# A second home for the shifted copy of g, convolution diagonals loaded from memory, and state scalars emitted inside the MLP

## The chip, the core and the metric

The kernel runs on one core of a Trainium2 chip. The metric is the device time of one execution in microseconds (us). Three runs of the kernel before took 1066.11, 1067.0 and 1065.13 us, median 1066.11. TensorE (PE) does the matrix products, VectorE (DVE) and ScalarE (ACT) the elementwise work, GpSimd (POOL) fills and small jobs; SP issues nearly all DMA.

## What is computed

Two blocks run one after the other on a sequence of 256 tokens with 1024 channels, in float32. The first block has two hybrid layers (sliding-window attention beside retention, gates, and an MLP with squared ReLU). The second has an "even" mixer (block attention and pooling) and an "odd" mixer, in which a state-space branch stands beside a convolution branch. Only the odd mixer is touched by what follows:

```python
def odd_mixer(h, w_in, ...):
    z = h @ w_in
    su, gc, ca, cb, gd = jnp.split(z, ...)          # 512 channels each
    y = s5_ssm(su, ...)                             # state branch
    ya, yb = jnp.split(y @ glu_w + glu_b, 2, axis=-1)
    ssm_out = ya * jax.nn.sigmoid(yb) * jax.nn.silu(gc)
    conv_out = conformer_conv(ca, cb, dw, ln_g, ln_b, pw) * jax.nn.silu(gd)
    return jnp.concatenate([ssm_out, conv_out], axis=-1) @ w_out

def conformer_conv(a, gl, dw, ln_g, ln_b, pw):
    g = a * jax.nn.sigmoid(gl)
    c = causal depthwise convolution of g, 31 taps per channel
    return silu(layernorm(c) * ln_g + ln_b) @ pw
```

## The kernel before

All weights stream through SP in 164 chunks, nearly all of 1 MB (`raw0` to `raw163`, three buffers, `fetch`, line 315). Each chunk is cut in two halves of 128x1024; ACT casts a half to `hi` (line 336) and DVE makes the rest `lo` (line 337), five buffers each, and every product is three matmuls of `hi` and `lo` parts. The Tile framework puts the instructions in order on each engine; code under `tc.high_priority(-N)` is moved towards the rear. Each engine, and SP with its DMA queue, works strictly in its own order.

The odd mixer takes the last 165 us and the chunks 147 to 163: `su` (147, 148), `cb` and `ca` of the two channel halves (149 to 152), `gc` and `gd` (153 to 156, all written to banks named `og`), the GLU weights (157 for `gb`, 158 for `ga`), then the output and point weights (159 to 163).

The convolution is done by TensorE. The gated input g is written into the tile `big` in two halves of 256 channels (line 1361). `strip(p)` (line 1326) makes a copy `g4[p]` in which the four partition groups hold g shifted by 0, 8, 16 and 24 tokens, with 16 DMAs of 65.8 KB each from SBUF to SBUF (line 1331). The copy of half 0 lies in the room of `pwc`, which the state branch reads until its output matrices `Q` are written (`s5_outputs`, line 1249, 16 small ACT operations, line 1207). The copy of half 1 lies in the room of `E`, which `states(0)` to `states(3)` (line 1292) read. `convolve(p)` (line 1341) then multiplies each channel group with diagonal 32x32 matrices of taps, 128 matmuls a half (line 1349), into a bank `cq`. The diagonals are made in eight pieces by POOL (`taps`, line 1334), three buffers, from the tap vectors in `pv` and an identity table `e32`.

`states(q)` is a DVE chain of products, two scans (line 1308, with a mask `Mt` from ACT and POOL) and products again, for four groups q; its results `wall` are read by the state output matmuls `ys` (line 1410), which follow the matmuls `ys` of the inner part (line 1403). Then come the means for the layer norm (`mu`, line 1390), `gb`, `ga` and the output product `yo`.

The large tiles named `xs` take turns in two rooms of 16 KB a partition: the normalized input of the odd mixer (read by `su` to `og`), `BT`, `Q`, and later `is_` and `fs` (inputs of the GLU and output products). The bank tag `sm` has four banks; the four `vb` banks that `states` reads hold all of them until each is read.

`after_mixer` (line 1519) closes the pool of the layer and emits the scalars of the state branch at low priority. It is called at line 830, ahead of the MLP of layer 1.

Of the kernel before, what the change touches and what calls it, by code (L numbers as in the profile page):

```python
# [152 lines left out]
def pack_weights(cs, inp):  # L153
# [3 lines left out]
    for blocks, n in zip(cs, w):  # L157
# [14 lines left out]


_PV = [("g_mix", 16), ("g_mlp", 16), ("g_final", 8), ("pre", 16), ("post", 16), ("pscale", 4), ("d", 4),
       ("glub", 8), ("dw", 16 * KP), ("lng", 4), ("lnb", 4), ("sinks", 16)]
PVO = {}
_o = 0
for _n, _w in _PV:
# [6 lines left out]
def strips(dw):  # L185

    t = np.zeros((4 * KP, 512), np.float32)
    t[:CONVK] = dw
    return t.reshape(4, KP, 4, 4, 32).transpose(0, 4, 2, 1, 3).reshape(P, 16 * KP)


def pack_vectors(inp):
    def v(a):
        return np.asarray(a, np.float32).reshape(-1, P).T

    cols = [v(inp["g_mix"]), v(inp["g_mlp"]), v(inp["g_final"]), v(inp["pre_norm_g_2"]), v(inp["post_norm_g_2"]),
            v(inp["e_pool_scale_2"]), v(inp["o_d_2"]), v(inp["o_glu_b_2"]),
            strips(inp["o_dw_2"][0]),
            v(inp["o_ln_g_2"]), v(inp["o_ln_b_2"]),
            np.broadcast_to(inp["sinks"].reshape(1, 16), (P, 16))]  # L200
    return np.ascontiguousarray(np.concatenate(cols, axis=1))


# [11 lines left out]
    return np.ascontiguousarray(np.concatenate(cols, axis=1))  # L215


_CT = [("ident", 128), ("mask0", 128), ("maske", 256), ("ecos", 64), ("esin", 64), ("blk", 128), ("icnt", 64), ("e32", 32)]
_MT = [("rcos", 256), ("rsin", 128), ("acos", 128), ("asin", 64), ("mask1", 256), ("dm", 1024)]
CTO = {}  # L220
_o = 0
# [8 lines left out]
def tables():  # L230
    t = np.zeros((P, NCT), np.float32)

    def put(name, a):
        t[:, CTO[name][0]:CTO[name][1]] = np.asarray(a, np.float64).reshape(P, -1)

    f32 = np.float32
    pos = np.arange(S, dtype=f32)

    def rope(inv):
        ang = (pos[:, None] * inv.astype(f32)[None, :]).astype(f32).astype(np.float64)  # L240
        c, s = np.cos(ang), np.sin(ang)
        return [a.reshape(NT, P, -1).transpose(1, 0, 2) for a in (np.concatenate([c, c], axis=1), s)]

    put("ident", np.eye(P))
    c, s = rope((10000.0 ** (-(np.arange(32) / 32.0))).astype(f32))
    put("acos", c)
    put("asin", s)
    theta = (1.0 / (10000.0 ** np.linspace(0.0, 1.0, 64))).astype(f32)
    c, s = rope(theta)
    put("rcos", c)  # L250
    put("rsin", s)
    c, s = rope((500000.0 ** (-(np.arange(0, 32, 2) / 32.0))).astype(f32))
    put("ecos", c)
    put("esin", np.concatenate([-s, s], axis=2))
    lg = np.log(1.0 - 2.0 ** (-5.0 - np.arange(4)))
    j, i = np.arange(P)[:, None], np.arange(P)[None, :]
    dm = np.zeros((P, 2, 4, P))
    for h in range(4):
        dm[:, 0, h] = np.where(i >= j, np.exp(lg[h] * np.maximum(i - j, 0)), 0.0)
        dm[:, 1, h] = np.exp(lg[h] * (i + P - j))  # L260
    put("dm", dm)
    q, k = np.arange(P)[:, None], np.arange(P)[None, :]
    put("mask0", np.where(k <= q, 0.0, NEG))
    k = np.arange(2 * P)[None, :]
    rel = q + P - k
    put("mask1", np.where((rel >= 0) & (rel < P), 0.0, NEG))
    put("maske", np.where(rel >= 0, 0.0, NEG))
    cnt = np.stack([np.minimum(np.arange(S) + 1, w) for w in (2, 4, 8, 16)])
    put("icnt", np.broadcast_to((1.0 / cnt)[None, :, :16], (P, 4, 16)))
    blk = np.zeros((P, 4, 32))  # L270
    for r in range(4):
        blk[32 * r:32 * r + 32, r] = 1.0
    put("blk", blk)
    put("e32", np.tile(np.eye(32), (4, 1)))
    return t


# [3 lines left out]
def build(ctx, tc, w, xin, pv_in, ct_in, s5_in, pg_in, out, parts=(0, 1, "e", "o"), dbg=None):  # L281
# [329 lines left out]
    def layer(l, xh, xl, norm, after_mixer, done):  # L611
# [215 lines left out]
            split_pair(xh2, xl2, x, "g_mlp", l * KT, p)  # L827
            n2.add(s)
        dump(f"xa{l}", x)
        after_mixer()  # L830


        def up(j, hook=None):
            hi, lo = chunk()
# [50 lines left out]

        bs = [up(0), up(1, square)]
        cur = up_out(bs[0])
        for j in range(16):
            if j + AHEAD < 16:
                bs.append(up(j + AHEAD))  # L890
            nxt = up_out(bs[j + 1]) if j < 15 else None
            if not accs:
                accs += [[bank("acc", f"dn{t}{h}") for h in range(2)] for t in range(NT)]
            hi, lo = chunk()
            if j < 15:
                for kk in range(2):
                    for t in range(NT):
                        for h in range(2):
                            down(j, cur, t, h, kk, hi, lo)
            else:  # L900
                ys = {}
                for h in range(2):
                    for t in range(NT):
                        for kk in range(2):
                            down(j, cur, t, h, kk, hi, lo)
                        ys[h, t] = w2("dny")
                        A.activation(ys[h, t], accs[t][h], AF.Copy, scale=r2[0][:, t:t + 1])
                        if h and t == 0:
                            back(0, [ys[0, 0], ys[0, 1]])
                back(1, [ys[1, 0], ys[1, 1]])  # L910
            cur = nxt
# [348 lines left out]
    def odd(pool, xh, xl, n, s5, tabs5):  # L1260
# [26 lines left out]
                                 start=True, stop=True)  # L1287
                vbs.append(vb)

        pg = pool.tile([P, D], F32, name="pg", tag="cd", bufs=1)  # L1290

        def states(q):
            vb = vbs[q]
            wt = wall[:, q]
            W.append(wt)
            ec, es = (E[:, a, 4 * q:4 * q + 4, :].rearrange("p r c -> p (r c)")[:, None, :].to_broadcast([P, 2, 4 * NC])
                      for a in range(2))
            tb = pool.tile([P, 2, 4 * NC], F32, name="tb", tag="tb", bufs=2)
            tt(wt, vb, ec, M)
            tt(tb, vb, es, M)  # L1300
            tt(wt[:, 0], wt[:, 0], tb[:, 1], AD)
            tt(wt[:, 1], wt[:, 1], tb[:, 0], SU)
            m = w2("Mt")[:, 0:4 * NC].rearrange("p (r c) -> p r c", r=4)
            A.copy(m, mL[:, 4 * q:4 * q + 4, None].to_broadcast([P, 4, NC]))
            G.memset(m[:, :, 0:1], 0.0)
            mf = m.rearrange("p r c -> p (r c)")
            for a in range(2):
                V.tensor_tensor_scan(wt[:, a], mf, wt[:, a], 0.0, M, AD)
            tb = pool.tile([P, 2, 4 * NC], F32, name="tb", tag="tb", bufs=2)
            tt(tb, wt, es, M)  # L1310
            tt(wt, wt, ec, M)
            tt(wt[:, 0], wt[:, 0], tb[:, 1], SU)
            stt(wt[:, 1], wt[:, 1], -1.0, tb[:, 0], M, SU)
# [11 lines left out]

        def strip(p):

            g4[p] = s5["pool"].tile([P, 2, 4, GS + 1], F32, name="g4", tag=("pwc", "E")[p], bufs=1)
            for s in range(4):
                for r in range(4):  # L1330
                    nc.sync.dma_start(g4[p][32 * s:32 * s + 32, :, r, 0:GS],
                                      g[32 * r:32 * r + 32, 2 * p:2 * p + 2, KP * s:KP * s + GS])

        def taps(q, h):
            n = 2 * KP
            o = PVO["dw"] + (2 * q + h) * n
            tap[q, h] = pool.tile([P, n, 32], F32, name="taps", tag="taps", bufs=3)
            G.tensor_tensor(tap[q, h], pv[:, o:o + n, None].to_broadcast([P, n, 32]),
                            C("e32")[:, None, :].to_broadcast([P, n, 32]), op=M)

        def convolve(p):
            b = bank("sm", "cq").rearrange("p (j t) -> p j t", j=2)
            for j in range(2):
                q = 2 * p + j
                for k in range(KP):
                    if k % 4 == 0:
                        taps(q, k // 4)
                    for r in range(4):
                        T.matmul(b[32 * r:32 * r + 32, j, :], tap[q, k // 4][:, 4 * (k % 4) + r, :],
                                 g4[p][:, j, r, k:k + S], start=k == 0, stop=k == KP - 1)  # L1350
            A.copy(cv[:, 2 * p:2 * p + 2, :], b)

        for p in range(2):
# [9 lines left out]
            if p == 0:  # L1363
                inputs()
                with tc.high_priority(-LOWW):
                    Q = s5_outputs(pool, s5)
                G.dma_start(pg, bass.AP(tensor=pg_in.tensor, offset=pg_in.offset, ap=[[0, P], [1, D]]))
        for i, d in enumerate((gc, gd)):
            with tc.high_priority(-LOWW):
                states(i)  # L1370
            for p in range(2):
                silu_gate(d[:, 2 * p:2 * p + 2, :], t_pair("acc", "og", xh, xl), R, 0.25)
        convolve(0)
        states(2)
        convolve(1)
        states(3)

        fh, fl, fs = twin("fs")
        ih, il, is_ = twin("is_")

        hb = pool.tile([P, 16], F32, name="hb")
# [40 lines left out]
        for p, b in enumerate(t_quad("acc", "gb", ih, il)):  # L1422
            for j in range(2):
                n = 2 * p + j
                th = w2("gth")[:, 0:S]
                A.activation(th, b[:, j, :], AF.Tanh, scale=0.5, bias=hb[:, 4 + n:5 + n])
                stt(gc[:, n, :], th, 1.0, gc[:, n, :], AD, M)
        gas = t_quad("acc", "ga", ih, il, hook=lambda: later.append(nv.rstd()))
        r3 = later.pop()
        for p, b in enumerate(gas):  # L1430
# [108 lines left out]
    for p in range(4):  # L1539
        n.add(x[:, 2 * p:2 * p + 2, :])  # L1540
    fetch()
    nc.sync.dma_start(pv[:, NG:], pv_in[:, NG:])
    nr = CTO["mask1"][0] - NCC
    nc.sync.dma_start(tabs[1][:, 0:nr], ct_in[:, NCC:NCC + nr])
    nc.sync.dma_start(ct, ct_in[:, 0:NCC])
# [117 lines left out]
```

## Time and profile before

| What | Value |
|---|---|
| median of three runs | 1066.11 us |
| time of the profiled execution | 1064.91 us |
| its span, first to last instruction | 1063.1 us |
| TensorE busy | 1025.0 us, 96% of the span |
| VectorE, ScalarE, GpSimd busy | 759.9, 547.1, 22.7 us |
| mean granted TensorE clock | 0.989 |
| moved by DMA | 179.05 MB, mean 168 GB/s |

The profiled execution is 1.2 us below the median, and 1.8 us of it lie outside the span. A row "A <- B: us, times, longest" in the view of waits says that A stood idle until B ended. In timelines and in the chain of waits the first column is the start, the second the time until the end of the piece, which may hold several equal instructions (xN).

### The profile page before, as it was taken

Reading aid. Unit: us, or ns where it says so; the run is one execution under the profiler, and the core shown is the slowest. Engines: PE = TensorE matmul, PEld = TensorE weight load, DVE = VectorE, ACT = ScalarE, POOL = GpSimd, SP = SyncE. Lnnn points to the kernel's source line nnn. Section 1 sums busy time; section 2 is a strip of 40 time slices with the busy share of each in tenths; the row PEclk is TensorE's granted clock in tenths of the full one; section 3 lists DMA queues with packets and bytes.
Section 4 is the critical chain, followed back from the end, with each engine's and each line's share of the span. In section 5 each row is a group of like instructions: output and inputs, shape, how many; then the busy total and the mean of one; then the engine's idle time right before and its main releaser. Section 6 shows DMA issues by size and latency. Waiting matters only on the chain.

```text
span 1063.1 us, 16059 instructions
## 1 busy us (share of the span) xinstructions
PE 1025.0 (96%) x6404; PEld 882.6 (83%) x6404; DVE 759.9 (71%) x1306; ACT 547.1 (51%) x844; POOL 22.7 (2%) x24
## 2 busy tenths in 40 slices
PE   7999999999999999999999999999999998995796
PEld 5887888988888888887888988888878998994595
DVE  6768656785666659478566999965677886879085
ACT  6545653554445455547544554445475557562052
POOL 0000000000000000000000000000000030012000
PEclk9999999999999999999999999999999999998799
DMA  9654445455555545544445555555545443444121
GB/s 333 227 175 154 159 138 180 163 195 196 181 198 176 198 171 186 198 158 153 153 149 193 171 194 198 176 199 179 198 153 182 151 159 121 150 139 176 35 80 40
DMA packets 29274, 179.05 MB, mean 168 GB/s; under 512 B 3600, under 2 KB 5776, under 8 KB 8592
## 3 DMA queue, kind: packets, MB, share of 16 engines
q1 hardware_dynamic: 28624, 176.44, 48.2%
q8 instruction: 50, 0.82, 0.3%
q0 software_dynamic: 288, 1.07, 0.3%
q10 hardware_dynamic: 288, 0.52, 0.1%
q14 instruction: 24, 0.20, 0.1%
HBM read 174.82 MB, written 1.05 MB: 165 GB/s over the span
## 4 chain that ended last, share of the span: by engine, by line
PE 91%; DVE 4%; ACT 2%; DMA 1%; issue 1%; SPq 1%; DVEq 0%; ACTq 0%
PE up L842 11%; PE ng L406 6%; PE ng L404 6%; PE ng L405 6%; PE up L843 6%; PE dn L865 5%; PE dn L864 5%; PE dn L866 5%; PE gate L404 3%; PE gate L406 3%; PE gate L405 3%; PE yb L406 1%; PE yb L404 1%; PE yb L405 1%; DVE lo L337 1%
## 5 line engine op out<-in xcount | busy, mean ns | idle before, releaser
L337 DVE TENSOR_TENSOR lo<-raw,hi 128x1024 fp32r<-128x1024 f32 (+1 forms) x331 | 399.1, 1210 | 188.8 <-ACT hi L336 187.2
L336 ACT CAST hi<-raw 128x1024 fp32r<-128x1024 f32 (+1 forms) x331 | 342.6, 1039 | 313.1 <-PE dn L866 81.7
L842 PE MATMUL up<-xs,hi 128*128 128x512 f32 x512 | 182.0, 398 | 0.8 <-DVE xs L465 0.8
L843 PE MATMUL up<-xs,lo 128*128 128x256 f32 x512 | 143.6, 280 | 0.0
L842 PEld LDWEIGHTS up<-xs,hi 128*128 128x128 f32 x512 | 96.2, 188 | 24.4 <-DVE xs L465 1.2
L404 PE MATMUL ng<-hi,xs 128*128 128x512 f32 x272 | 108.4, 399 | 8.2 <-ACT xs L464 8.2
L405 PE MATMUL ng<-lo,xs 128*128 128x512 f32 x272 | 107.0, 393 | 0.0
L406 PE MATMUL ng<-hi,xs 128*128 128x512 f32 x272 | 106.7, 394 | 0.1
L864 PE MATMUL dn<-hi,uph 128*128 128x512 f32 x256 | 100.1, 391 | 0.0
L865 PE MATMUL dn<-lo,uph 128*128 128x512 f32 x256 | 99.9, 390 | 0.0
L866 PE MATMUL dn<-hi,upl 128*128 128x512 f32 x256 | 99.6, 389 | 0.0
L843 PEld LDWEIGHTS up<-xs,lo 128*128 128x128 f32 x512 | 96.7, 189 | 1.0
L404 PEld LDWEIGHTS ng<-hi,xs 128*128 128x128 f32 x272 | 51.6, 190 | 18.9 <-ACT xs L464 8.7
L406 PEld LDWEIGHTS ng<-hi,xs 128*128 128x128 f32 x272 | 51.3, 189 | 11.8 <-DVE xs L465 1.0
L405 PEld LDWEIGHTS ng<-lo,xs 128*128 128x128 f32 x272 | 51.7, 190 | 10.6
L864 PEld LDWEIGHTS dn<-hi,uph 128*128 128x128 f32 x256 | 48.1, 188 | 10.5
L866 PEld LDWEIGHTS dn<-hi,upl 128*128 128x128 f32 x256 | 48.1, 188 | 10.2
L865 PEld LDWEIGHTS dn<-lo,uph 128*128 128x128 f32 x256 | 48.1, 188 | 8.9
L404 PE MATMUL gate<-hi,xs 128*128 128x512 f32 x128 | 51.6, 403 | 0.0
L406 PE MATMUL gate<-hi,xs 128*128 128x512 f32 x128 | 49.9, 390 | 0.0
L405 PE MATMUL gate<-lo,xs 128*128 128x512 f32 x128 | 49.9, 390 | 0.0
L850 ACT COPY upa<-up 128x256 f32<-128x256 f32 x64 | 23.7, 370 | 47.8 <-PE up L843 47.8
(382 smaller groups left out, 1920.5 us busy)
## 6 DMA issues: line engine op xcount, KB each, us to landing
raw<-w_dram SPq DMA_DIRECT2D x161, 1024.0 KB, 4.9
raw<-w_dram SPq DMA_DIRECT2D x9, 256.0 KB, 5.6
g<-big SPq DMA_DIRECT2D x32, 65.8 KB, 2.0
x<-x_dram SPq DMA_DIRECT2D x4, 256.0 KB, 5.7
ctm<-ct_dram SPq DMA_DIRECT2D x1, 640.0 KB, 10.1
sp<-s_dram POOLq DMA_DIRECT2D x1, 536.0 KB, 4.0
pg<-pg_dram POOLq DMA_DIRECT2D x1, 512.0 KB, 3.7
out_dram<-xn SPq DMA_DIRECT2D x2, 256.0 KB, 2.0
```

The source lines that it names most:

```text
L336: A.copy(hi[:, s], raw[:, rs])
L337: V.tensor_tensor(lo[:, s], raw[:, rs], hi[:, s].bitcast(F32), op=OP.subtract)
L404: T.matmul(b[t], xh[:, k, ts], hi[:, ws], start=f, stop=False)
L405: T.matmul(b[t], xh[:, k, ts], lo[:, ws], start=False, stop=False)
L406: T.matmul(b[t], xl[:, k, ts], hi[:, ws], start=False, stop=e)
L842: T.matmul(bs[i], hi[:, ws], xs2[:, k], start=k == 0, stop=False, skip_group_check=True)
L843: T.matmul(bs[i][:, 1, :], lo[:, ws], xh2[:, k, :], start=False, stop=k == KT - 1, skip_group_check=True)
L850: A.copy(u[:, j, :], b[:, 0, :])
L864: T.matmul(accs[t][h], th[:, kk, tk], hi[:, ws], start=f, stop=False)
L865: T.matmul(accs[t][h], th[:, kk, tk], lo[:, ws], start=False, stop=False)
L866: T.matmul(accs[t][h], tl[:, kk, tk], hi[:, ws], start=False, stop=e)
```

## The change

The second copy of g gets a tile of its own, `g4`, in the pool of the odd mixer; the room comes from the three buffers of diagonals and one of the two buffers `tb`, which go. The diagonals come ready-made from memory, behind the vectors in `pv_dram`: four loads of 512 KB. They lie in the old room of `sp` (q=0), in that of `cd` (q=1), and in one of the two `xs` rooms (q=2 and 3), and are issued by POOL, POOL, SP and ACT. The row `pg`, which lay in the room of `cd`, is loaded behind the convolution. `fs` is allocated later. The call of `after_mixer` stands behind the first products of the MLP.

```diff
@@ strips: taps on the diagonals of 32x32 blocks
-    return t.reshape(4, KP, 4, 4, 32).transpose(0, 4, 2, 1, 3).reshape(P, 16 * KP)
+    t = t.reshape(4, KP, 4, 4, 32).transpose(0, 2, 1, 3, 4)
+    z = np.zeros((4, 32, 4, KP, 4, 32), np.float32)
+    for c in range(32):
+        z[:, c, ..., c] = t[..., c]
+    return z.reshape(P, 512 * KP)
@@ layer
         dump(f"xa{l}", x)
-        after_mixer()
...
         bs = [up(0), up(1, square)]
         cur = up_out(bs[0])
+        after_mixer()
@@ states (twice)
-            tb = pool.tile([P, 2, 4 * NC], F32, name="tb", tag="tb", bufs=2)
+            tb = pool.tile([P, 2, 4 * NC], F32, name="tb", tag="tb", bufs=1)
@@ strip
-            g4[p] = s5["pool"].tile([P, 2, 4, GS + 1], F32, name="g4", tag=("pwc", "E")[p], bufs=1)
+            n = 2 * 4 * (GS + 1)
+            if p == 0:
+                t = s5["pool"].tile([P, n], F32, name="g4", tag="pwc", bufs=1)
+            else:
+                t = pool.tile([P, n], F32, name="g4", tag="g4", bufs=1)
+            g4[p] = t.rearrange("p (j r t) -> p j r t", j=2, r=4)
@@ taps
-        def taps(q, h):
-            n = 2 * KP
-            o = PVO["dw"] + (2 * q + h) * n
-            tap[q, h] = pool.tile([P, n, 32], F32, name="taps", tag="taps", bufs=3)
-            G.tensor_tensor(tap[q, h], pv[:, o:o + n, None].to_broadcast([P, n, 32]),
-                            C("e32")[:, None, :].to_broadcast([P, n, 32]), op=M)
+        def taps():
+            n = KP * P
+            late = acts.tile([P, 4 * n], F32, name="taps", tag="xs", bufs=2)
+            for q in range(4):
+                if q < 2:
+                    home, tag = ((s5["pool"], "sp"), (pool, "cd"))[q]
+                    t = home.tile([P, n], F32, name="taps", tag=tag, bufs=1)
+                else:
+                    t = late[:, (q - 2) * n:(q - 1) * n]
+                (G, G, nc.sync, nc.scalar)[q].dma_start(t, pv_in[:, NPV + q * n:NPV + q * n + n])
+                tap[q] = t.rearrange("p (n c) -> p n c", c=32)
@@ odd, from the first half of g on
-                G.dma_start(pg, bass.AP(tensor=pg_in.tensor, offset=pg_in.offset, ap=[[0, P], [1, D]]))
...
+        taps()
         convolve(0)
         states(2)
         convolve(1)
         states(3)
-        fh, fl, fs = twin("fs")
+        pg = pool.tile([P, D], F32, name="pg", tag="cd", bufs=1)
+        G.dma_start(pg, bass.AP(tensor=pg_in.tensor, offset=pg_in.offset, ap=[[0, P], [1, D]]))
         ih, il, is_ = twin("is_")
...
+        fh, fl, fs = twin("fs")
         gas = t_quad("acc", "ga", ih, il, hook=lambda: later.append(nv.rstd()))
```

The order of the SP queue in the odd mixer before, from the last `gd` chunk on; `g4_8660` is the copy of half 0, `g4_8857` that of half 1:

```order
L325 DMA raw156_8952<-w_dram 128x2048
L325 DMA raw157_9030<-w_dram 128x2048
L1331 DMA g4_8660<-big_8533 32x2x263 x16
L325 DMA raw158_9093<-w_dram 128x2048
L325 DMA raw159_9509<-w_dram 128x2048
L325 DMA raw160_9581<-w_dram 128x2048
L325 DMA raw161_9672<-w_dram 128x2048
L1331 DMA g4_8857<-big_8533 32x2x263 x16
L325 DMA raw162_9729<-w_dram 128x2048
L325 DMA raw163_9763<-w_dram 128x2048
```

and the same place of the same queue after the change, with `g4_8659` for half 0, `g4_8855` for half 1 and the diagonals of q=2:

```order
L327 DMA raw156_8950<-w_dram 128x2048
L1335 DMA g4_8659<-big_8532 32x2x263 x16
L1335 DMA g4_8855<-big_8532 32x2x263 x16
L327 DMA raw157_9028<-w_dram 128x2048
L327 DMA raw158_9091<-w_dram 128x2048
L1348 DMA taps_9154<-pv_dram 128x1024
L327 DMA raw159_9499<-w_dram 128x2048
L327 DMA raw160_9572<-w_dram 128x2048
L327 DMA raw161_9663<-w_dram 128x2048
```

Both copies of g now stand ahead of the GLU weights (157, 158), and the diagonals of q=2 stand behind these.

TensorE's order before, from the end of the `og` products on (`cq` is the convolution's bank, `ys` the state output's):

```order
L1349 MATMUL cq_9156<-g4_8660,taps_9211 32x256 x16
L1349 MATMUL cq_9245<-g4_8857,taps_9246 32x256 x2
L1403 MATMUL ys_9340<-uP_8371,K_8087 128x256
L1349 MATMUL cq_9245<-g4_8857,taps_9246 32x256
L1403 MATMUL ys_9340<-uP_8371,K_8087 128x192
L1349 MATMUL cq_9245<-g4_8857,taps_9246 32x256 x13
L1349 MATMUL cq_9245<-g4_8857,taps_9264 32x256 x16
```

and after it:

```order
L1357 MATMUL cq_9161<-g4_8659,taps_9155 32x256 x32
L1357 MATMUL cq_9161<-g4_8659,taps_9157 32x256 x32
L1357 MATMUL cq_9242<-g4_8855,taps_9154 32x256 x64
L1412 MATMUL ys_9330<-uP_8371,K_8087 128x256
L1412 MATMUL ys_9330<-uP_8371,K_8087 128x192
L1412 MATMUL ys_9330<-uP_8371,K_8087 128x128
```

The two halves of the convolution now follow each other whole, and all `ys` products stand behind them. (A matmul here stands for two instructions of the trace.) Outside the odd mixer no engine's order of computing instructions is changed but for POOL's, which loses the making of the diagonals.

## Rows read from the trace of the kernel before

**Rows 1.** Waits of PE, 895 to 1064 us: us in total, times, longest

```profile
PE cq L1349 <- DMA g<-big: 17.8, 1, 17.8
```

**Rows 2.** Chain that ended last, around that wait: start, us, what

```profile
980.63 0.43 DVE wall L1042
981.06 0.15 SPq L1331
...
987.64 0.59 SPq L1331
988.28 2.02 DMA g<-big
990.30 0.14 issue
990.44 1.69 PE cq L1349 x4
```

**Rows 3.** Timeline of PE around the convolution

```profile
965.48 7.14 PE L1349 MATMUL cq<-g,taps 128*32 128x256 f32 x128
990.44 1.69 PE L1349 MATMUL cq<-g,taps 128*32 128x256 f32 x4 [17.82 <-DMA g<-big]
...
1003.89 1.97 PE L1410 MATMUL ys<-wall,Q 128*32 128x63 f32 x128
1005.78 2.62 PE L1403 MATMUL ys<-uP,K 128*128 128x256 f32 x16
1008.33 1.97 PE L1410 MATMUL ys<-wall,Q 128*32 128x63 f32 x128
...
1011.87 0.47 PE L391 MATMUL gb<-is__9335,hi 128*128 128x256 f32 x1
```

**Rows 4.** Stretches: length, busy us (instructions) by engine, granted clock, DMA share, GB/s

```profile
930.00:965.00 35.00, 35.00 (x294) 35.00 (x294) 27.02 (x42) 19.76 (x33) 4.38 (x5) 1.00 0.54 177
959.00:967.00 8.00, 8.00 (x83) 7.28 (x85) 7.77 (x14) 3.58 (x6) 0.00 (x0) 1.00 0.95 361
972.60:990.40 17.80, 0.02 (x3) 0.00 (x0) 8.68 (x15) 0.59 (x1) 2.06 (x1) 0.65 0.22 53
990.40:1003.90 13.50, 13.46 (x146) 7.84 (x147) 0.00 (x0) 0.59 (x1) 1.05 (x1) 0.83 0.06 13
```

**Rows 5.** Timeline of SP's queue in the odd mixer

```profile
945.40 12.64 SPq L1331 DMA_DIRECT2D g<-big  x16
958.15 10.75 SPq L325 DMA_DIRECT2D raw<-w_dram  x4
980.62 10.18 SPq L1331 DMA_DIRECT2D g<-big  x16
```

**Rows 6.** Timelines of POOL and ACT where Q is made

```profile
931.61 0.60 POOL L1367 DMA_DIRECT2D pg<-pg_dram  x1 [31.60 <-PE vb L1286]
932.21 3.57 POOL L1253 MEMSET Q<- 128x2048 f32 x2
934.07 1.27 ACT L1207 ACTIVATE Q<-pwc 64x256 f32<-64x256 f32 x3 [7.68 <-POOL Q L1253]
944.90 0.42 ACT L1207 ACTIVATE Q<-pwc 64x256 f32<-64x256 f32 x1
```

**Rows 7.** Timeline of DVE: g's second half, and the end of the states

```profile
946.53 0.69 DVE L1051 SCALAR_TENSOR_TENSOR big<-cth,ca 128x512 f32<-128x512 f32 x1
980.97 0.42 DVE L1051 SCALAR_TENSOR_TENSOR wall<-wall,tb 128x256 f32<-128x256 f32 x1
```

**Rows 8.** Issue to landing: weight chunks from 900 us on, then the copies of g

```profile
DMA to landing us min/median/max: 4.7/4.8/8.1
DMA to landing us min/median/max: 2.0/2.0/7.1
```

**Rows 9.** The page's DMA issues: times, KB each, us to landing

```profile
sp<-s_dram POOLq DMA_DIRECT2D x1, 536.0 KB, 4.0
pg<-pg_dram POOLq DMA_DIRECT2D x1, 512.0 KB, 3.7
```

**Rows 10.** Timeline of ACT: the cast of chunk 160

```profile
1019.02 1.05 ACT L336 CAST hi<-raw 128x1024 fp32r<-128x1024 f32 x1
```

More of the change, by code (lines that the diff above doesn't have):

```diff
@@ L174 @@
 _PV = [("g_mix", 16), ("g_mlp", 16), ("g_final", 8), ("pre", 16), ("post", 16), ("pscale", 4), ("d", 4),
-       ("glub", 8), ("dw", 16 * KP), ("lng", 4), ("lnb", 4), ("sinks", 16)]
+       ("glub", 8), ("lng", 4), ("lnb", 4), ("sinks", 16)]
 PVO = {}
@@ L197, in pack_vectors @@
             v(inp["e_pool_scale_2"]), v(inp["o_d_2"]), v(inp["o_glu_b_2"]),
-            strips(inp["o_dw_2"][0]),
             v(inp["o_ln_g_2"]), v(inp["o_ln_b_2"]),
-            np.broadcast_to(inp["sinks"].reshape(1, 16), (P, 16))]
+            np.broadcast_to(inp["sinks"].reshape(1, 16), (P, 16)), strips(inp["o_dw_2"][0])]
     return np.ascontiguousarray(np.concatenate(cols, axis=1))
@@ L215, in pack_s5 @@
     return np.ascontiguousarray(np.concatenate(cols, axis=1))
-_CT = [("ident", 128), ("mask0", 128), ("maske", 256), ("ecos", 64), ("esin", 64), ("blk", 128), ("icnt", 64), ("e32", 32)]
+_CT = [("ident", 128), ("mask0", 128), ("maske", 256), ("ecos", 64), ("esin", 64), ("blk", 128), ("icnt", 64)]
 _MT = [("rcos", 256), ("rsin", 128), ("acos", 128), ("asin", 64), ("mask1", 256), ("dm", 1024)]
@@ L273, in tables @@
     put("blk", blk)
-    put("e32", np.tile(np.eye(32), (4, 1)))
     return t
@@ L1288, in inputs @@
                 vbs.append(vb)
-        pg = pool.tile([P, D], F32, name="pg", tag="cd", bufs=1)
         def states(q):
@@ L1308, in states @@
                 V.tensor_tensor_scan(wt[:, a], mf, wt[:, a], 0.0, M, AD)
-            tb = pool.tile([P, 2, 4 * NC], F32, name="tb", tag="tb", bufs=2)
+            tb = pool.tile([P, 2, 4 * NC], F32, name="tb", tag="tb", bufs=1)
             tt(tb, wt, es, M)
@@ L1345, in convolve @@
                 for k in range(KP):
-                    if k % 4 == 0:
-                        taps(q, k // 4)
                     for r in range(4):
-                        T.matmul(b[32 * r:32 * r + 32, j, :], tap[q, k // 4][:, 4 * (k % 4) + r, :],
+                        T.matmul(b[32 * r:32 * r + 32, j, :], tap[q][:, 4 * k + r, :],
                                  g4[p][:, j, r, k:k + S], start=k == 0, stop=k == KP - 1)
@@ L1541, in build @@
     fetch()
-    nc.sync.dma_start(pv[:, NG:], pv_in[:, NG:])
+    nc.sync.dma_start(pv[:, NG:], pv_in[:, NG:NPV])
     nr = CTO["mask1"][0] - NCC
```

## The prediction

> **What bounds the kernel now.** The table of the page says that TensorE (PE) is busy for 96% of the span, so a change can give time back only where PE stands idle or runs at a lower clock, and can cost time wherever it makes PE wait. The view of waits, cut to the odd mixer, leaves one such place: PE stands for 17.8 us ahead of line 1349 until a transfer of the shifted copy of g has landed [rows 1]. The chain that ended last shows which transfer [rows 2]: DVE's last product of `states(3)` ends at about 981, SP then issues the 16 DMAs of the second copy, the last lands 2.02 us after its issue, and PE starts. The second copy waits for `states(3)` because it lies in the room of `E`. PE's own timeline shows what surrounds the gap [rows 3]: the first half of the convolution takes 7.14 us at 965.48 to 972.62; the second half begins at 990.44; state output products of line 1403 are mixed into it; and the first product of line 1410 starts at 1003.89. Last, the stretches [rows 4]: from 930 to 965 PE is busy for 35.00 of 35 us at full clock, so nothing is to be won there; in the gap the granted clock falls to a mean of 0.65, and in the 13.5 us behind it, with PE busy for 13.46, it is 0.83. The gap thus costs twice, as a wait and as a cold restart.
>
> **The change part by part.** I compare one stretch of PE: from the start of the first half of the convolution (965.48) to the first product of line 1410 (1003.89), 38.41 us [rows 3]. The products in it are the same before and after: two halves of 128 instructions and 16 instructions `ys` of line 1403 (the other 16 come behind).
>
> Second copy in a home of its own: it waits no more for `states(3)`. Both copies now wait for g alone and, in the first one's case, for the last `Q` operation. After that, PE's stretch is first half, second half, 16 instructions of line 1403, warm: 7.14 + 7.14 + 2.55 (line 1403 at 1005.78 to the next row at 1008.33) = 16.83, plus whatever wait w remains ahead of the second half. Saving 38.41 - 16.83 - w = 21.58 - w. It consists of the 17.82 wait and of 3.76 that the cold, mixed stretch of 13.45 (990.44 to 1003.89) took above 7.14 + 2.55 = 9.69.
>
> When do the copies go? POOL fills `Q` at 932.21, after 0.60 for issuing `pg` [rows 6]; `pg` now goes behind the convolution, and the two loads that POOL issues instead stand well before the fill and behind it. The fill begins at some 931.0, and the last `Q` operation (before: 944.90 + 0.42 = 945.32) ends about as much earlier; after 1.9 of fill as before (932.21 to 934.07, rows 6) ACT starts at 932.9; 16 operations of 0.42 with two casts of 1.05 and a gate of some 0.6 between them end at 942.3, which I take for the first issue. The copy of half 0 reads g's first half, there long before; the second copy comes after 16 issues, so g's second half at 947.2 [rows 7] is no wait either. The issue of 16 took 12.64 us at 945.40, beside weight traffic, and 10.18 at 980.62 [rows 5], 0.79 and 0.64 us each. 32 at the lower price are 20.4 us, so SP has issued both copies at 962.7; at the higher, 25.3 and 967.6. The second copy lands 2 to 7 us behind its last issue [rows 8], at about 965 in the first case, long before 972.6, when the second half needs it.
>
> Diagonals loaded: q=0 and q=1, 512 KB each, take the room of `sp` and `cd`, whose readers are done before, and land while PE works off `su` to `og`. At the 361 GB/s that the busiest stretch shows [rows 4] they are 1.5 us each of a DMA system that is busy for 0.54 of 930 to 965; loads of that size from POOL landed in 4.0 and 3.7 us [rows 9]. I price them at nothing; PE's work, fed by chunks already there, is the cover. q=2 and q=3 lie in the room that `og`'s products read until 965.3, just ahead of the convolution's 965.48. They can be issued then, no sooner, and are needed at 965.48 + 7.14 = 972.62. Here the change adds a wait. The load of q=2 stands on SP behind the strips and two weight chunks: the strips end at 962.7, chunk 157 goes out at about 963, 158 0.7 later, so it leaves at 965.6, with ACT's q=3 beside it. 2 x 1.05 MB and 2 x 0.52 MB, 3.15 MB in all, are 8.7 us at 361 GB/s. A chunk lands 4.8 us behind its issue [rows 8], of which 2.9 are bytes at that rate, so 1.9 is the way: 962.9 + 1.9 + 8.7 = 973.5 for the last, w = 0.9. The lower bound is 0 (as `pg`, 3.7 us behind its issue, 969.3). The upper one has the strips at 12.64 each: queue free at 967.6, load landed at 967.6 + 0.4 + 1.9 + 8.7 = 978.6, w = 6.0. The row for the wait's two ends that stands nearest is the copy beside weight chunks (7.1 us at most instead of 2.0, rows 8): 965.6 + 7.1 = 972.7. I take w = 1.0. What waits behind this DMA on SP are chunks 159 to 161. Chunk 160 is not cast before 1019.02 [rows 10], 998.4 after a shift of 20.6, and would land near 980. The GLU chunk 157, now behind 32 strips instead of ahead of 16, lands at about 968; `gb` needs it at 1011.87 - 20.6 = 991.3 [rows 3]. So both have 18 us or more in hand.
>
> On this wait a rule speaks against the change. The trace shows that copies of 2.0 us took up to 7.1 when weight chunks were ahead of them [rows 8]. The Trainium skill, "DMA: Bandwidth & Descriptors", section "Queues, rings and completion order", says that a DMA engine takes a queue's descriptors in ring order, and turns between queues packet by packet. By it the load of q=2, 4 KB a partition behind two chunks, ends only behind their bytes (w near 1), while the one on ACT shares with them. Without it both would land like `pg`, and w would be 0. The trace agrees with the rule as far as the 7.1 goes; no row of before has a load behind two chunks.
>
> Diagonals no longer made on POOL: POOL is busy for 22.7 us in all, and PE does not wait for it in the odd mixer [rows 1], so this is worth nothing (bounds 0 and a gain of some 0.5, where POOL works beside DVE). One `tb` buffer instead of two: writer and reader are both DVE, which goes in its own order, 0 (bounds -0.5 to 0.5, off the path). `states(3)` ended at 980.97 + 0.42 = 981.39 [rows 7]; its result is needed by line 1410 at 965.48 + 16.83 + 1 = 983.3. With 2 us in hand this is what is late next: DVE's queue now holds three casts of chunk 157 and the first of 158 behind the scans, and a chunk that is late there holds `states(3)`. `pg` lands near 977 and is not read before the layer norm's end. Scalars emitted inside the MLP: no engine's order differs outside the odd mixer but for POOL's missing products, so 0.
>
> Sum: 21.58 - 1.0 = 20.6. The profiled execution takes 1064.91, its span 1063.1: the changed kernel's 1044.3 and 1042.5. The median of the runs is 1.2 above the profiled execution, so 1045.5; I take 1045.0, between these two.
>
> **The rivals.** *The load behind the chunks is late* (chance 0.20). Strips at the price beside weight traffic, w = 3 to 6, and PE restarts cold, which costs up to the 3.76 above again: 1066.11 - 21.58 + 3 = 1047.5 at the least, 1066.11 - 21.58 + 6.0 + 3.76 = 1054.3 at the most, 1050 in the middle. For it: the first strip did take 12.64 beside weights. Against it: SP's queue has no weight chunk between raw156 and the strips' end. The same times hold when DVE is what is late: `states(3)` held by a cast of a late chunk 157, PE waiting ahead of line 1410 for 2 to 4 us.
>
> *The change does not do what it says* (0.02). If the second copy waited for another room's reader, or g's second half itself were late, the gap would stay: 1064 to 1066. Against it: the order of SP's queue has the two copies back to back, and g is whole at 947.2 [rows 7].
>
> *Slower* (0.03). One mechanism: the loads of q=2 and q=3 take rows of 4 KB that lie far apart in memory, issued only at 965.6, behind chunks; should they be slow, PE stands ahead of the second half as before, in the same place, with the price of w. It decides from w = 21.58, a landing at 994.2, 28.6 us behind the issue; at 32 the time would be 1069.5. Against it: `sp` and `pg`, of the same size, took 4.0 and 3.7 [rows 9].
>
> *Forecast* (0.75): w from 0 to 3, 1044.5 to 1047.5, and down to 1042.5 if the profiled execution rather than the median is the measure and every bound below zero counts.
>
> **How the numbers follow.** The time is that of the forecast, 1045.0, its own range 1042.5 to 1047.5. To hold 8 in 10, with the share of late loads taken in up to the middle of that rival: 1042.0 to 1051.0. A measurement of this kernel tells about 0.2% (2.1 us) from no change. Faster by more: 0.75 + 0.20 = 0.95; within: 0.02; slower: 0.03.
>
> **What would show it.** In the profile after, the 17.8 wait for `g<-big` is gone, both halves of the convolution stand back to back on PE with at most 3 us between, waiting for `taps`, not for g; SP's strips are one run of 32 from 942 to 963, the last `Q` operation ends near 942; the granted clock from 965 to 983 stays near 1.00; the first product of line 1410 starts near 983, `gb` near 991. It is wrong if PE waits for 6 us or more ahead of the second half, if a new wait stands ahead of line 1410, or if `gb` waits for chunk 157.

## The result

The changed kernel takes 1049.17 us (median of 4 runs, 1046.61 to 1050.58) against 1066.55 for the kernel before in the same session: ratio 0.9835, 95% interval 0.9812 to 0.9858, 17.4 us less. The forecast was 1045.0. The profiled execution took 1048.67 us with a span of 1046.7, against 1064.91 and 1063.1 before: 16.4 us less of span. One experiment below (e1) was profiled in an execution disturbed from end to end, 2627 us; that time and profile are left out, and the kernel was profiled again.

Waits of PE in the changed kernel, from 895 us on (the row that answers to [rows 1]):

```profile
PE cq L1357 <- DMA taps<-pv_dram: 3.5, 1, 3.5
```

The wait of 17.8 for g is gone. A new one stands in its place, of 3.5 us, for the loaded diagonals. Timeline of PE around the convolution (compare [rows 3]):

```profile
965.65 7.14 PE L1357 MATMUL cq<-g,taps 128*32 128x256 f32 x128
976.25 8.72 PE L1357 MATMUL cq<-g,taps 128*32 128x256 f32 x128 [3.47 <-DMA taps<-pv_dram]
984.91 2.62 PE L1412 MATMUL ys<-uP,K 128*128 128x256 f32 x16
987.46 1.97 PE L1419 MATMUL ys<-wall,Q 128*32 128x63 f32 x128
...
995.44 0.47 PE L393 MATMUL gb<-is__9325,hi 128*128 128x256 f32 x1
```

From the start of the first half to the first product of `wall` and `Q` it is now 987.46 - 965.65 = 21.81 us, where before it was 38.41: 16.60 saved, which is the whole of the gain in the span. From there to the end both kernels take 59.2 us. The second half took 8.72 instead of the 7.14 of the first, though its instructions are the same.

The stretches show why (columns as in [rows 4]):

```profile
930.00:965.00 35.00, 35.00 (x294) 35.00 (x294) 26.04 (x40) 16.73 (x29) 4.23 (x5) 1.00 0.42 118
...
972.60:976.30 3.70, 0.23 (x5) 0.08 (x2) 3.67 (x6) 2.58 (x3) 0.53 (x1) 0.93 1.03 423
976.30:985.00 8.70, 8.70 (x129) 8.29 (x129) 5.44 (x7) 1.04 (x1) 0.00 (x0) 0.83 0.86 320
```

While PE waits, the DMA system is full (share 1.03, 423 GB/s), and behind the wait the granted clock is 0.83 in the mean: PE restarts cold, as after the long wait of before. In finer stretches the clock, 1.00 until 975.75, is 0.50 (1.2 GHz) from 976.25 to 979.0, PE having stood still from 972.8 to 976.25, 0.79 from 979.0 to 979.5, and 1.00 (2.4 GHz) from there on.

The chain that ended last, up to that wait, then SP's queue in the same place (compare [rows 2, 5]):

```profile
941.95 0.42 ACT Q L1208
...
964.78 0.54 SPq L327
965.41 0.39 SPq L327
965.90 10.22 DMA taps<-pv_dram
...
976.25 8.72 PE cq L1357 x128
```

```profile
942.43 22.25 SPq L1335 DMA_DIRECT2D g<-big  x32
964.78 1.02 SPq L327 DMA_DIRECT2D raw<-w_dram  x2
965.90 0.38 SPq L1348 DMA_DIRECT2D taps<-pv_dram  x1
966.37 13.23 SPq L327 DMA_DIRECT2D raw<-w_dram  x3
```

The 32 copies hold SP until 964.7. Only then do chunks 157 and 158 go out, and the diagonals of q=2 right behind them. Issues and landings of 960 to 980 (copies, KB each, us to landing):

```profile
raw<-w_dram SPq DMA_DIRECT2D x5, 1024.0 KB, 7.1
taps<-pv_dram ACTq DMA_DIRECT2D x1, 512.0 KB, 8.7
taps<-pv_dram SPq DMA_DIRECT2D x1, 512.0 KB, 10.2
```

DVE is not late: its last product of `states(3)` is done at 980.64 (compare [rows 7]). That is 6.8 us before PE's first products of `wall` at 987.46, and these read only q=0 and q=1; q=2 and q=3 are read by the second run of such products, from 991.90 on.

```profile
980.22 0.42 DVE L1052 SCALAR_TENSOR_TENSOR wall<-wall,tb 128x256 f32<-128x256 f32 x1
```

### The profile page after: what moved, and what is told of

It reads as the page before. It is cut to its first block, busy times and chain, and to the rows that moved or that the text cites. A ratio compares the mean times of both kernels' runs of the same rounds, so it can differ in the third digit from the quotient of the medians.

```text
span 1046.7 us, 16046 instructions
## 1 busy us (share of the span) xinstructions
PE 1022.0 (98%) x6404; PEld 885.1 (85%) x6404; DVE 756.5 (72%) x1306; ACT 546.7 (52%) x844; POOL 11.0 (1%) x18
## 4 chain that ended last, share of the span: by engine, by line
PE 90%; DVE 3%; ACT 2%; DMA 2%; issue 1%; SPq 1%; DVEq 0%; ACTq 0%
PE up L842 11%; PE ng L408 6%; PE ng L406 6%; PE ng L407 6%; PE up L843 6%; PE dn L865 6%; PE dn L864 6%; PE dn L866 6%; PE gate L406 3%; PE gate L408 3%; PE gate L407 3%; PE yb L407 1%; PE yb L408 1%; PE yb L406 1%; DVE lo L339 1%
## 5 line engine op out<-in xcount | busy, mean ns | idle before, releaser
L407 PEld LDWEIGHTS ng<-lo,xs 128*128 128x128 f32 x272 | 51.9, 191 | 10.6
L866 PEld LDWEIGHTS dn<-hi,upl 128*128 128x128 f32 x256 | 48.1, 188 | 10.2
```

Of the source, the lines that this page charges most:

```text
L407: T.matmul(b[t], xh[:, k, ts], lo[:, ws], start=False, stop=False)
L866: T.matmul(accs[t][h], tl[:, kk, tk], hi[:, ws], start=False, stop=e)
```

## The experiments

Theory: the own home of the second copy brings the whole gain, and the two weight chunks ahead of the diagonals, in time if not in the queue, cost the 3.5 us and the cold restart. Rivals: loads of diagonals that are slow by themselves; queue order alone; DVE or POOL as a hidden source of the gain.

**e1, e1b: the diagonals ahead of the chunks.** One edit of the changed kernel:

```diff
-                (G, G, nc.sync, nc.scalar)[q].dma_start(t, ...)
+                with tc.high_priority(1500 if q == 2 else 0):
+                    (G, G, nc.sync, nc.scalar)[q].dma_start(t, ...)
```

> The changed kernel with one edit: on SP the load of the diagonals q=2 stands ahead of the weight chunks 157 and 158 (and of the last of the 32 copies) instead of behind them. Theory: the 3.47 us for which PE waited ahead of the second half are the bytes of the two chunks, 2 x 1.05 MB, ahead of the load in SP's queue. Then q=2 is issued at about 965.6 as before, lands about 970.5, PE does not wait, the second half runs warm in 7.14 instead of 8.72, and the time is 3.5 + 1.6 = 5.0 us less than the changed kernel's: about 17.4 + 5.0 = 22.4 less than the kernel before, about 1044. Rival: the load is slow by itself (rows of 4 KB that lie 17 KB apart in memory); then it lands near 976 again, PE waits 3 to 3.5, and the time stays 17.4 less than before's, about 1049.

> The kernel of e1_diag_first once more, for a profile of its usual execution and a second time of it: with the load of q=2 ahead of chunks 157 and 158 the times were 1042.9 to 1044.5, 2.1% below before. Theory: the profile shows no wait ahead of the second half, the load landed by 971, the second half warm in 7.1, the first product of line 1419 some 17 us after the convolution's start instead of 21.8, and chunks 157 and 158 landed before 976, with no wait at gb. Time 1043 to 1045. Rival: PE still waits there for 1 us or more and the gain came from elsewhere.

Measured: 1044.14 us, ratio 0.9788 (0.9775 to 0.9802), and 1044.09, ratio 0.9800 (0.9787 to 0.9813). Of e1b PE's timeline, SP's queue, and issues and landings:

```profile
966.21 14.05 PE L1358 MATMUL cq<-g,taps 128*32 128x256 f32 x256
980.19 2.62 PE L1413 MATMUL ys<-uP,K 128*128 128x256 f32 x16
982.74 1.97 PE L1420 MATMUL ys<-wall,Q 128*32 128x63 f32 x128
```

```profile
966.31 0.35 SPq L1349 DMA_DIRECT2D taps<-pv_dram  x1
966.70 0.59 SPq L1335 DMA_DIRECT2D g<-big  x1
967.39 15.99 SPq L327 DMA_DIRECT2D raw<-w_dram  x5
```

```profile
taps<-pv_dram SPq DMA_DIRECT2D x1, 512.0 KB, 5.2
taps<-pv_dram ACTq DMA_DIRECT2D x1, 512.0 KB, 5.4
```

The load lands in 5.2 us instead of 10.2, the two halves run as one block of 14.05, and the stretch is 982.74 - 966.21 = 16.53 instead of 21.81. The loads are not slow by themselves; the theory holds. The chunks land later than expected (158 at 979.6, not before 976), but nobody waits at `gb`.

**e2: the diagonals of q=2 in a queue of their own.**

```diff
-                (G, G, nc.sync, nc.scalar)[q].dma_start(...)
+                (G, G, G, nc.scalar)[q].dma_start(...)
```

> The changed kernel with one edit: the diagonals q=2 are issued by POOL (its own DMA queue) instead of SP; the chunks 157 and 158 still go out at 964.8 and 965.4. It tells queue order from shared bandwidth. Theory (the load waits for its turn in SP's queue): beside the chunks instead of behind them it gets a share, lands at 970 to 973, PE waits 0 to 0.5, time 4 to 5 us less than the changed kernel's, about 1044 to 1045. Rival (the bytes of all four transfers share the DMA engines, whatever the queue): it lands with the others at 975 to 976, PE waits 2.5 to 3.5, time about 1048 to 1049. The load of q=3 on ACT's queue took 8.7 us, which speaks for the rival.

Measured: 1049.62 us, ratio 0.9845 (0.9831 to 0.9859). Its wait of PE, and its landings:

```profile
PE cq L1357 <- DMA taps<-pv_dram: 4.6, 1, 4.6
```

```profile
taps<-pv_dram ACTq DMA_DIRECT2D x1, 512.0 KB, 11.4
taps<-pv_dram POOLq DMA_DIRECT2D x1, 512.0 KB, 11.3
```

SP's queue in this run:

```profile
964.92 14.98 SPq L327 DMA_DIRECT2D raw<-w_dram  x5
```

Queue order alone falls: with neither load in SP's queue, both came in as late as behind the chunks. But the run changes two things: SP, rid of the load, sends chunk 159 at 966.04, ahead of ACT's load (966.07) and POOL's (966.33). ACT's load, whose queue is the same in both kernels, took 11.4 us here and 8.7 in the changed kernel. So the third chunk, with the load on POOL, cost up to 2.7 us, and what POOL's load would have taken without it is not shown. The changed kernel itself gives a cleaner reading: there q=3, on ACT's own queue and behind two chunks only, landed at 974.45, 1.7 us sooner than q=2 and still 1.7 us later than the 972.8 at which PE wanted q=2. By these landings an own queue would have saved about half of the wait (an estimate); the rest goes with what was issued before, on whatever queue.

**e7: one chunk more ahead of the load.**

```diff
+                if q == 2:
+                    nc.sync.dma_start(late[:, 2 * n:], chunk_dram(158))
                 (G, G, nc.sync, nc.scalar)[q].dma_start(...)
```

> The changed kernel with one transfer more: 1 MB from the weights into the unused half of the diagonals' room, on SP just ahead of the load of q=2; nothing reads it. It doubles the suspected cost. Theory (bytes ahead of the load): at 361 to 400 GB/s the load lands 2.6 to 2.9 us later, PE waits 6.1 to 6.4 instead of 3.5, and the restart is no dearer than 1.6 to 3.8: the time is 2.6 to 5 above the changed kernel's, 1052 to 1054. Rival (the load's own time sets it): as the changed kernel, 1049, to 1050.

Measured: 1052.78 us, ratio 0.9876 (0.9859 to 0.9894), 3.6 above the changed kernel's time, or 4.4 by the two ratios. PE's second half:

```profile
980.62 9.47 PE L1359 MATMUL cq<-g,taps 128*32 128x256 f32 x128 [7.71 <-DMA taps<-pv_dram]
```

The load lands 4.4 us later than in the changed kernel's profile; 0.7 of that is SP, whose copies ended at 965.4 in this execution, and 3.7 comes with the one megabyte more, above the 2.6 to 2.9 expected; the wait grew to 7.7 and not to 6.1 to 6.4.

**e3: the second copy issued by POOL.**

```diff
-                    nc.sync.dma_start(g4[p][32 * s:32 * s + 32, ...
+                    (nc.sync, G)[p].dma_start(g4[p][32 * s:32 * s + 32, ...
```

> The changed kernel with one edit: the 16 DMAs of the second copy are issued by POOL instead of SP. SP is then free near 953, chunks 157 and 158 go out near 954 and land by 962, and the load of q=2 stands behind chunks 159 and 160 instead, of which one or both go out just before 965.5. Theory (what counts is the bytes under way when the load starts, 3.15 MB in the changed kernel): with about one chunk less, 2.1 MB, the load lands at 971 to 974, PE waits 0 to 1.5, time 1043.5 to 1046. Rival (the copies are slower from POOL's queue): at more than 1 us each, or landing late behind chunks, the second copy lands after 973 and PE waits for g instead, time above 1048.

Measured: 1044.16 us, ratio 0.9797 (0.9783 to 0.9811). PE and POOL:

```profile
966.23 14.05 PE L1357 MATMUL cq<-g,taps 128*32 128x256 f32 x256
...
982.76 1.97 PE L1419 MATMUL ys<-wall,Q 128*32 128x63 f32 x128
```

```profile
948.29 8.48 POOL L1335 DMA_DIRECT2D g<-big  x16 [2.87 <-DVE big L1052]
```

POOL issues the 16 copies at 0.53 us each; SP sends chunk 157 at 954.16, and by the time that the diagonals may go, 157 and 158 are in (960.7 and 965.6). Chunks 159 and 160, issued at 957.19 and 964.19, are still under way; the load behind them took 5.5 us. The stretch is the same 16.53 as in e1b, by the other way: not the load is moved, but the two chunks right ahead of it. Both, with e7, say that the new wait is SP's 32 copies pushing two chunks into the moment of the load.

**e5: the home alone, diagonals made by POOL as before,** in the rooms of the changed kernel (not shown: the tap vectors and the table `e32`, which this needs, come back):

```diff
-                (G, G, nc.sync, nc.scalar)[q].dma_start(t, ...)
+                for h in range(2):
+                    G.tensor_tensor(tap[q][:, h * m:h * m + m], pv[...], C("e32")[...], op=M)
```

> The second copy in its own home without loaded diagonals: POOL makes the eight pieces as in the kernel before, in the rooms of the changed kernel (sp, cd, the xs room); four of them ahead of time, the four of q=2 and 3 from 965.5 on. It tells whether the loads are needed for the gain. If the gain is the home alone, and POOL needs the 1.55 us a piece of the kernel before: q=2 is ready at 968.7, q=3 at 971.8, PE needs them at 972.8 and 976.4, no wait, second half warm, and the time is that of the kernel before less 21 to 22: about 1044 to 1045, 4 to 5 below the changed kernel. Rival: POOL beside DVE slows both (2 us and more a piece, the scans of states later), PE waits 1 to 4 ahead of the second half or ahead of the state outputs: 1046 to 1049.

Measured: 1045.66 us, ratio 0.9804 (0.9791 to 0.9817).

```profile
968.10 14.05 PE L1359 MATMUL cq<-g,taps 128*32 128x256 f32 x256
982.08 2.62 PE L1414 MATMUL ys<-uP,K 128*128 128x256 f32 x16
984.63 1.97 PE L1421 MATMUL ys<-wall,Q 128*32 128x63 f32 x128
```

Again 16.53, with no load at all. (This execution reached the convolution 2.4 us later; the granted clock was 0.91 from 880 to 900 and 0.94 from 900 to 930, against 1.00 in the changed kernel.) The gain needs the home, not the loads; in the changed kernel the loads cost some 3 to 4 us.

**e4: the loads without the home.**

```diff
-            if p == 0:
-                t = s5["pool"].tile([P, n], F32, name="g4", tag="pwc", bufs=1)
-            else:
-                t = pool.tile([P, n], F32, name="g4", tag="g4", bufs=1)
+            t = s5["pool"].tile([P, n], F32, name="g4", tag=("pwc", "E")[p], bufs=1)
```

> The changed kernel with the second copy of g back in the room of E; the diagonals are loaded and the rest is as changed. It tells whether the loads and the other edits are worth anything without the home. Theory (all of the gain is the home): the second copy waits for states(3) again, which ends near 980 to 981, PE waits 17 to 18 us ahead of the second half, time 1063 to 1067, within 0.2% of before. Rival (the loads free DVE of POOL's work and the states end earlier): states(3) ends 2 to 5 us earlier than 981, time 1060 to 1064.

Measured: 1063.11 us, ratio 0.9976 (0.9966 to 0.9986), 2.6 less than before. Wait of PE and the end of DVE's states in e4, then scans of DVE and POOL's work in the kernel before:

```profile
PE cq L1354 <- DMA g<-big: 15.3, 1, 15.3
```

```profile
974.71 1.27 DVE L1307 TENSOR_TENSOR_SCAN wall<-Mt,wall 128x256 f32<-128x256 f32 x2
...
977.81 0.42 DVE L1052 SCALAR_TENSOR_TENSOR wall<-wall,tb 128x256 f32<-128x256 f32 x1
```

```profile
969.92 2.92 DVE L1308 TENSOR_TENSOR_SCAN wall<-Mt,wall 128x256 f32<-128x256 f32 x2
```

```profile
969.46 2.84 POOL L1338 TENSOR_TENSOR taps<-pv,ct 128x512 f32<-128x512 f32 x2
```

Here the rival is right. Without POOL's work beside it, two scans take 1.27 us instead of 2.92, `states(3)` ends at 978.2 instead of 981.4, and so the wait is 15.3 instead of 17.8. Once the copy has a home of its own, this is off the path and worth nothing.

**e6: the scalars' call in its old place.**

```diff
+        after_mixer()
         ...
         cur = up_out(bs[0])
-        after_mixer()
```

> The changed kernel with the call that emits the scalars of the state branch back in its old place, ahead of the MLP's first products. Theory: the engines' orders are the same, so the time is the changed kernel's, 1047 to 1050.5, and the wait ahead of the second half 3 to 4. Rival (the place matters through what waits there): off by more than 2 us either way.

Measured: 1048.29 us, ratio 0.9834 (0.9820 to 0.9848), against 0.9835 of the whole change; the wait was 3.3. This part of the change does nothing that can be measured.

**e8, e9: does chunk 159, issued behind the load, delay it?** In e8 SP loads `pg` between the load and chunk 159; e9 is the changed kernel on the same chip.

```diff
-        G.dma_start(pg, ...)
+        with tc.high_priority(1000):
+            nc.sync.dma_start(pg, ...)
```

> The changed kernel with one edit: the row pg is loaded by SP instead of POOL, between the load of q=2 and chunk 159. It must wait for the first half of the convolution (972.8), so chunk 159, which went out at 966.4, half a us behind the load of q=2, goes out after 973. The other engines' orders are unchanged. It asks why q=2 landed at 976.1 when the bytes of chunks 157, 158, q=2 and q=3, 3.15 MB at the 418 GB/s seen from 968 to 976, would be in by about 974.3. Theory: chunk 159, though issued behind the load on the same queue, took some 0.8 MB of the transfer ahead of its last bytes; then q=2 lands at 974 to 974.6, PE waits 1.3 to 2 instead of 3.5, and the time is 1.5 to 2.5 below the changed kernel's. Rival (a queue delivers in its own order, so 159 cannot matter): q=2 lands at 976 as before, wait 3.3 to 3.6, time unchanged.

> The changed kernel as it is, as a second profile and a time on the same chip as e8. All theories: wait ahead of the second half 3.3 to 3.6 for the diagonals, the second half 8.7 to 9.2, time 1047 to 1050.5.

Measured: e8 1049.65 us, ratio 0.9841 (0.9828 to 0.9855); e9 1050.48, ratio 0.9852 (0.9839 to 0.9866). SP's queue of e8, and its second half; then the same of e9:

```profile
943.35 23.36 SPq L1335 DMA_DIRECT2D g<-big  x32
966.81 1.02 SPq L327 DMA_DIRECT2D raw<-w_dram  x2
967.92 0.69 SPq L1348 DMA_DIRECT2D taps<-pv_dram  x1
973.74 0.33 SPq L1387 DMA_DIRECT2D pg<-pg_dram  x1
```

```profile
977.79 8.62 PE L1357 MATMUL cq<-g,taps 128*32 128x256 f32 x128 [4.12 <-DMA taps<-pv_dram]
```

```profile
943.22 23.31 SPq L1335 DMA_DIRECT2D g<-big  x32
966.63 1.02 SPq L327 DMA_DIRECT2D raw<-w_dram  x2
```

```profile
978.22 10.08 PE L1357 MATMUL cq<-g,taps 128*32 128x256 f32 x128 [4.68 <-DMA taps<-pv_dram]
```

My theory of 0.8 MB taken by chunk 159 falls. From the issue of chunk 157 to PE's restart it is 11.0 us with 159 held, and with it 11.6 in e9, 11.5 in the changed kernel's first profile and 11.4 in e6, so 159 costs about 0.5 and not 1.5 or more. The time difference, 0.8 us, lies inside the intervals. The clear part of e9 is another: the copies began 0.8 us later and took 23.3 us, so chunk 157 went out at 966.6, the load was later by as much, and the wait rose to 4.7.

## Why the prediction came out as it did

The time lies in the range given (1042 to 1051), but not in the likeliest case's own (1042.5 to 1047.5): what happened is the rival "the load behind the chunks is late", chance 0.20, at its lower end. The range held because it took in the lower half of that rival.

- *The wait for g and the mixed restart go.* Right. With no other wait the stretch is 16.53 us (e1b, e3, e5); the forecast had 16.83. The time of e1b, 1044.1, is what the forecast gives with w at 0, 1044.0.
- *First issue of the copies at 942.3.* Right: 942.43.
- *32 copies at 0.64 us each, queue free at 962.7.* This step failed. I took the price of the quiet stretch of before, the lower end of what the rows gave (0.64 to 0.79, [rows 5]), for a place in which part of the time weights still move. It was 22.25 us, 0.70 each, in this execution and 0.73 in e9. Chunk 157 left at 964.78 and not at 962.9.
- *10.6 us from there to the landing of q=2 (way and bytes).* Nearly right, by luck: 976.1 - 964.8 = 11.3. The rate of 361 GB/s was too low; from 968 to 976 it was 418, at which 3.15 MB are 7.5 us and not 8.7, so that way and bytes would have ended at about 974.2. Of the 1.9 us left, chunk 159 explains about 0.5 (e8); the rest stays open. Together the two steps make w 3.47 where I took 1.0.
- *The restart behind a short wait.* Left out of the forecast and counted only in the rival: 8.72 - 7.14 = 1.58. The shortfall in the stretch, 20.6 - 16.6 = 4.0, is 2.5 of wait and 1.6 of cold clock. The granted clock did not stay near 1.00 until 983 as I wrote; it was 0.83 from 976.3 to 985.
- *The rule on queue order.* The Trainium skill, "DMA: Bandwidth & Descriptors", "Queues, rings and completion order": a DMA engine takes a queue's descriptors in ring order. The trace agrees as far as the load behind two chunks took 10.2 us and a chunk behind it cost it little (e8). But ring order does not explain the wait alone: q=3, in a queue of its own, took 8.7 us behind the same two chunks, and leaving SP's queue did not help (e2, 11.3, with a third chunk ahead). The section's other statement, turns between queues packet by packet, gave neither load a share that brought it in by 972.8.
- *POOL's work removed, worth nothing (0 to 0.5).* Right for the sum, since DVE is off the path; wrong about the size: where DVE is on the path, the change without the home is worth 2.6 us (e4), and the scans show POOL's part in it.
- *DVE next to be late, 2 us in hand; chunk 157 in time for `gb`; scalars' place 0.* The margin of 2 us was misread: I took the first products of `wall` for those that need `states(3)`, but they read q=0 and q=1, and q=3 is read only by the second run, 4.4 us later. In e3 `states(3)` ended at 983.11, 0.35 us after the first of these products (982.76), and PE did not wait. In e1b and in the changed kernel it ended 3.4 and 6.8 us before them. Chunk 157 landed at 969.8 and `gb` did not wait, and e6 shows 0.

In e1b and e5 PE also stands for 1.4 and 1.5 us inside the products of `wall` and `Q`, which the profile ascribes to no other engine, and in e3 it does not. DVE is not the cause: `states(3)` ended some 9 and 5 us earlier. What it is stays open.

## What to carry to other kernels

When a wait of one transfer is removed, look at what goes out in the same microseconds: here 32 small copies kept the queue until the moment at which the newly needed load could go, and two megabytes that TensorE first read more than 20 us later went first. Issue what is needed next ahead of it, or move the copies to an idle queue; either gave another 4 to 5 us. A wait of some 3 to 8 us on TensorE is to be priced with its restart, which cost about 1.5 to 3 more here.

## What the runs showed of the hardware

- **Order of issue counted across queues.** The load of q=3 on ACT's queue took 8.7 us where it was issued at 965.75, behind chunks 157 (964.78) and 158 (965.41) on SP's queue, and 8.0 in e7, issued 0.4 us behind 157 and 0.2 ahead of 158. In e8 and e9 ACT issued it just ahead of chunk 157 (in e9 at 966.51 and 966.63), and it took 3.7 and 3.8. The order is not strict: in e2 chunk 159, issued 0.03 us ahead of ACT's load, landed at 979.0, behind it (977.5). Of e9:

```profile
taps<-pv_dram ACTq DMA_DIRECT2D x1, 512.0 KB, 3.8
```

- **A short wait cools the clock unevenly.** After waits of 3.35 (e6), 3.47, 4.12, 4.61 (e2), 4.68 and 7.71 us the second half took 9.13, 8.72, 8.62, 8.59, 10.08 and 9.47 instead of 7.14. The level is the same each time, 0.50 (1.2 GHz); what differs is how long it lasted once PE worked again, 2.75 us in the changed kernel's first profile and some 5 in e9.
- **POOL and DVE slowed each other in the kernel before.** While POOL made diagonals, two scans of DVE took 2.92 us instead of 1.27, and POOL's pieces there took 1.4 to 2.1 each. In e5 POOL made four pieces in 4.54 us, 1.1 each, while DVE stood idle for more than half of that time; of the two DVE products beside them one took 1.27 instead of the 0.69 that it takes elsewhere, the other its usual 0.69:

```profile
968.26 4.54 POOL L1350 TENSOR_TENSOR taps<-pv,ct 128x512 f32<-128x512 f32 x4 [11.55 <-PE og L393]
```
